# VectorE's program in the first part of a one-core decoder trunk: an order from a play-through of all recorded operations in place of the scheduler's own

## The chip, the cores and the metric

The kernel runs on one core of one Trainium2 chip. A core has five engines that each work through a program of their own: TensorE (PE) for matmuls and its weight loads (PEld), VectorE (DVE), ScalarE (ACT), GpSimd (POOL) and SyncE (SP), which here mostly starts DMA transfers. They wait for one another through semaphores. The metric is the device time of one execution in microseconds (us), the median of several runs.

## The reference

One inference step of a decoder layer for two groups of requests that share the weights: one prompt of 1024 tokens, and 8 samples of 8 tokens each. Cut to what matters:

```python
h = rms_norm(x) * (1 + sc) + sh                       # adaLN of the condition c
P = h @ w_in                                          # 1024 -> 1792 rwkv + 512 pool + 2048 gate columns
r, k, v, xw, xa, xg = split(pr + (pr_prev - pr) * mu) # token shift
decay = exp(-exp(-softplus(-(w0 + tanh(xw) @ w2)) - 0.5))
# per head (8 heads of 64), per token:
S = S * decay + (S @ -kk) (kk * a)^T + v k^T          # 64 x 64 state
y = S @ r                                             # then group norm, bonus, gate g
o_p = grouped causal means over windows 2, 4, 8, 16, minus the token, @ pool_w
merged = sigmoid(g_r) * (y @ w_br_rwkv) + sigmoid(g_p) * (o_p @ w_br_pool)
x = x + gate * (merged @ w_out)
x = x + gate2 * (square(relu(adaLN(x) @ w_ff1)) @ w_ff2)
y = rms_norm(x)
```

All is float32. The new states (shift, pool and rwkv) are outputs too.

## The kernel before, in words

Features lie on the 128 partitions and tokens on the free axis: 1024 prompt tokens and 64 sample tokens make 1088 columns, cut in three chunks of 364, 362 and 362 for the matmuls. Large products are made of three matmuls in the type fp32r: an operand is split in a rounded part and a rest (`whi`/`wlo` for weights, pairs of `hx` rows for activations), and `mm3` adds hi·hi, hi·lo and lo·hi in PSUM. A weight block `wraw` (128x512) is loaded by SP, ACT makes `whi` of it, DVE makes `wlo = wraw - whi`; the first product with a `wlo` so waits for DVE.

The span has three stages. Up to about 95 us the condition's modulation, the norm and the first rows are made. From about 95 to 750 us runs `phase1`, the first part. Then `phase2` does the merge, `w_out`, and the MLP.

In `phase1` two kinds of work share PE. The **background** is a stream of projections (`stream`, `products`): for each block of columns of `w_in` it issues 8 x 3 x 3 matmuls into PSUM tiles of the tag `mm`; ACT and DVE evacuate them to rows `px`, then `d` (token shift) and to scratch in DRAM (`d_x`, `d_th`). The **foreground** are chains of small steps for four pairs of heads, f = 0 to 3:

- `front` and `ra`: k, kk, a, the decays by a scan along 64-token pieces (`wt`, `e`, `bk`, `ra`);
- `scores` (`unit`): the 64x64 products inside each piece (`ab`, `at`, `ak`), transposes of v (`uv`, loaded from `d_x` with 32x32 blocks exchanged);
- `inverse` and `level`: the inverse of a triangular 64x64 matrix for each piece, by a serial chain of fifteen pairs of DVE operations (`hv`, `tt`), then transposes (`iv`, `hv`) and small matmuls `w<-iv,hv`;
- `affine`, then `chain`: the state `S` goes through 16 pieces; at each, PE does `wc<-S,ra`, DVE does one small update `S<-S,end,wc`, and PE needs that `S` for the next;
- `sample` (the 8 x 8 sample tokens) and `post` (group norm by `w<-wt,bones`, reciprocals, bonus, gate).

The order of PE is written out when the program is built: `Pace.run` draws from the background and lets in a step of the foreground when a model of the engines (`Clocks`) says that its operands are there. Inside `manual_schedule(engines={PE})` PE keeps that order. DVE, ACT, POOL and SP are ordered by the tile scheduler, which takes instructions in its own view of readiness.  All DVE, ACT, POOL and SP operations go through the wrapper `Engine.__getattr__`, so in the profile before they all show the wrapper's line L187; PE's matmuls show L359.

Buffers come in rings of few places (`hv`, `iv`, `wt`, `ra`, `S` with 3, PSUM tag `mm` with 4, `w` and `wc` with 2): an operation that writes a new tile also waits until the old tile at that place has been read.

Of the kernel before, what the change touches and what calls it, by code (L numbers as in the profile page):

```python
# [10 lines left out]
F32R = mybir.dt.float32r  # L11
# [67 lines left out]
class Clocks:  # L79
# [5 lines left out]
    def __init__(self, pace):  # L85
        self.pace, self.on = pace, False
        self.busy = {"vector": [], "scalar": [], "gpsimd": [], "sync": []}
        self.seen, self.slots, self.table = {}, {}, 0

    def region(self, ap):  # L90
# [82 lines left out]


class Engine:

# [4 lines left out]
    def __getattr__(self, op):  # L181
        f = getattr(self.real, op)

        def g(*a, **kw):
            if self.c.on:
                self.c.op(self.name, op, a, kw)
            return f(*a, **kw)  # L187

        return g
# [11 lines left out]
class Pool:  # L201
# [5 lines left out]
    def tile(self, *a, **kw):  # L207
        t = self.pool.tile(*a, **kw)
        if self.c.on and kw.get("tag") and kw["tag"] not in self.free:
            self.c.new(kw["tag"], kw["bufs"], t)  # L210
        return t
# [110 lines left out]
class K:  # L322
# [27 lines left out]
    def mm(self, out, lhsT, rhs, **kw):  # L350
        n, mode = math.prod(rhs.shape[1:]), tuple(32 if v <= 32 else 64 if v <= 64 else 128 for v in (lhsT.shape[0], math.prod(lhsT.shape[1:])))
        if mode != self.mode:
            self.pace.t += 150 if self.clocks.on else 200
# [4 lines left out]
        self.product(out, lhsT, rhs)  # L358
        return self.nc.tensor.matmul(out, lhsT, rhs, **kw)  # L359

# [21 lines left out]
    def tr(self, out, in_, ident):  # L382
        if self.mode != (P, P):
            self.pace.t += 150 if self.clocks.on else 200
        self.mode = (P, P)
        if self.clocks.on:
            self.pace.t = max(self.pace.t, self.clocks.ready(in_), self.clocks.touch(out, False))
        self.pace.t += 2 * math.prod(ident.shape[1:]) / 2.4 + 3
        self.product(out, in_)
        self.nc.tensor.transpose(out, in_, ident)  # L390

# [1063 lines left out]
    def phase1(self, ctx):  # L1455
# [41 lines left out]
        self.orr = [[None] * 4 for _ in range(2)]  # L1497
        self.clocks.on = True
        self.pace.split = lambda: self.mode != (P, P)
        self.pace.run(back, [self.chains(), self.heads(), self.pools(), self.or_rows()])  # L1500
        self.clocks.on = False
        self.pace.split = lambda: True
        nc.scalar.dma_start(io["o_ns"], self.ns)
# [705 lines left out]
```

## Time and profile before

| | us |
|---|---|
| median of 3 runs (lowest, highest) | 1596.3 (1594.35, 1600.01) |
| profiled execution, its own time | 1603.45 |
| its span | 1601.7 |
| PE busy | 1536.2 (96%) |
| DVE busy | 1109.6 (69%) |
| ACT busy | 664.1 (41%) |
| POOL busy | 151.4 (9%) |

The rows of a profile name an instruction by line, engine, operation and tiles (`out<-in`, buffer numbers left out). "Idle before" is the time for which the engine had nothing to run ahead of that instruction, and the arrow names what ended it. In a table of windows the columns are the window, its length, the busy time of PE, PEld, DVE, ACT and POOL with the number of instructions, then the mean granted clock of PE (1.00 is full speed), the share of the DMA engines and GB/s. A list of a stretch in order of time gives start, duration, engine, and at the end in brackets the idle time before. The profiled execution took 7 us longer than the median of the runs.

### The profile page before, as it was taken

The page shows a single profiled execution, that of the slowest core. Times are in us where ns is not written, and L with a number is a line of the kernel's source. Part 1 is how long each engine was busy: PE and PEld are TensorE (multiplying, and loading weights), DVE is VectorE, ACT ScalarE, POOL GpSimd, SP SyncE. Part 2 cuts the span into 40 slices and gives each one's busy share as a digit, 9 for nine tenths or more (in the row PEclk, how much of TensorE's full clock was granted, in tenths as well). Part 3 has the DMA queues.
Part 4 walks back from the last instruction along what each step waited for, and adds up shares of the span by engine and source line. Part 5 has one row for each costly group of instructions (what it writes and reads, how often), then busy time and mean ns, then how long its engine had stood idle before and what let it go on. Part 6 is the DMA issues. An engine that isn't in the chain of part 4 may idle for free.

```text
span 1601.7 us, 34054 instructions
## 1 busy us (share of the span) xinstructions
PE 1536.2 (96%) x13777; PEld 1445.8 (90%) x13777; DVE 1109.6 (69%) x1944; ACT 664.1 (41%) x1287; POOL 151.4 (9%) x234
## 2 busy tenths in 40 slices
PE   4999999999998999999999999999999999999997
PEld 2998888988898879989899999999999999999997
DVE  5575658775877487536543797998767796666776
ACT  5454364455334543523222573222334344334652
POOL 3100000000000000012510120000000050000000
PEclk9999999999999999999999999999999999999998
DMA  9142523233333343855875555666445996664654
GB/s 363 62 135 76 181 84 112 80 131 128 95 127 119 99 125 119 304 198 179 305 270 188 194 170 198 226 212 206 144 151 202 400 350 197 210 195 160 227 175 144
DMA packets 136399, 290.05 MB, mean 181 GB/s; under 512 B 36881, under 2 KB 40977, under 8 KB 136241
## 3 DMA queue, kind: packets, MB, share of 16 engines
q1 hardware_dynamic: 129856, 266.75, 48.4%
q10 hardware_dynamic: 4320, 14.00, 2.7%
q0 software_dynamic: 2064, 7.13, 1.3%
q8 instruction: 108, 1.77, 0.4%
q14 instruction: 51, 0.41, 0.1%
HBM read 210.54 MB, written 77.28 MB: 180 GB/s over the span
## 4 chain that ended last, share of the span: by engine, by line
PE 79%; DVE 9%; DMA 6%; issue 2%; ACT 2%; SPq 1%; POOL 0%; DVEq 0%; ACTq 0%; POOLq 0%
PE mm L359 52%; PE w L359 13%; PE wc L359 13%; DVE wt L187 2%; DVE hx L187 2%; DMA hid<-in_w_ff 1%; DVE wlo L187 1%; SPq L187 1%; DMA mg<-in_w_ff 1%; DMA wt<-d_x 1%; DMA hid<-in_w_ada_mlp 1%; DVE hv L187 1%; DMA uv<-d_x 1%; DMA t<-d_th 1%; PE w L390 1%
## 5 line engine op out<-in xcount | busy, mean ns | idle before, releaser
L359 PE MATMUL mm<-hx,whi 128*128 128x362 f32 (+2 forms) x2944 | 690.3, 322 | 9.6 <-ACT px L187 3.6
L359 PEld LDWEIGHTS mm<-hx,whi 128*128 128x128 f32 x2944 | 497.9, 190 | 34.6 <-issue 12.8
L359 PE MATMUL mm<-hx,wlo 128*128 128x362 f32 (+2 forms) x1472 | 464.2, 315 | 4.5 <-DVE wlo L187 3.7
L359 PEld LDWEIGHTS mm<-hx,wlo 128*128 128x128 f32 x1472 | 279.6, 190 | 4.7 <-DVE wlo L187 4.7
L359 PE MATMUL mm<-mg,whi 128*128 128x272 f32 (+2 forms) x1312 | 248.8, 289 | 1.2 <-ACT whi L187 0.7
L359 PEld LDWEIGHTS mm<-mg,whi 128*128 128x128 f32 x1312 | 205.4, 188 | 6.1 <-issue 3.4
L359 PE MATMUL mm<-mg,wlo 128*128 128x272 f32 (+2 forms) x656 | 188.5, 287 | 0.0
L359 PE MATMUL wc<-hx,whi 128*128 128x272 f32 x896 | 170.4, 288 | 0.0
L187 ACT ACTIVATE whi<-hid 128x512 fp32r<-128x512 f32 x128 | 80.5, 630 | 148.5 <-PE mm L359 56.1
L359 PEld LDWEIGHTS wc<-hx,whi 128*128 128x128 f32 x896 | 140.3, 188 | 0.0
L359 PE MATMUL wc<-hx,wlo 128*128 128x272 f32 x448 | 128.9, 288 | 2.3 <-DVE wlo L187 2.3
L359 PEld LDWEIGHTS mm<-mg,wlo 128*128 128x128 f32 x656 | 123.6, 188 | 0.0
L187 DVE TENSOR_TENSOR wlo<-hid,whi 128x512 fp32r<-128x512 f32 x128 | 87.5, 686 | 41.0 <-ACT whi L187 40.3
L187 DVE TENSOR_TENSOR wlo<-wraw,whi 128x512 fp32r<-128x512 f32 x82 | 58.3, 711 | 66.7 <-ACT whi L187 60.6
L187 ACT ACTIVATE whi<-wraw 128x512 fp32r<-128x512 f32 x100 | 62.6, 627 | 90.6 <-PE mm L359 48.6
L359 PE MATMUL w<-hx,whi 128*128 128x272 f32 (+1 forms) x480 | 97.2, 297 | 0.0
L187 POOL TENSOR_TENSOR hx<-hx,rs 128x64 f32<-128x64 f32 x24 | 36.8, 1534 | 568.6 <-DMA mg<-in_w_ff 374.2
L359 PEld LDWEIGHTS wc<-hx,wlo 128*128 128x128 f32 x448 | 84.2, 188 | 2.8 <-DVE wlo L187 2.8
L359 PEld LDWEIGHTS w<-hx,whi 128*128 128x128 f32 x480 | 77.3, 189 | 1.0 <-issue 1.0
L359 PEld LDWEIGHTS mm<-mg,hx 128*128 128x128 f32 x576 | 72.8, 188 | 5.0 <-issue 5.0
L359 PE MATMUL mm<-mg,hx 128*128 128x272 f32 (+2 forms) x576 | 74.7, 289 | 0.0
L187 ACT ACTIVATE px<-mm 128x362 f32<-128x362 f32 (+3 forms) x113 | 46.3, 434 | 63.0 <-PE mm L359 56.4
(289 smaller groups left out, 2323.3 us busy)
## 6 DMA issues: line engine op xcount, KB each, us to landing
t<-d_t SPq DMA_DIRECT2D x56, 544.0 KB, 5.0
hid<-in_w_ff SPq DMA_DIRECT2D x110, 256.0 KB, 4.1
d_t<-hx SPq DMA_DIRECT2D x102, 272.0 KB, 2.5
hid<-in_w_ff SPq DMA_DIRECT2D x42, 512.0 KB, 3.8
wraw<-in_w_in SPq DMA_DIRECT2D x68, 256.0 KB, 2.8
mg<-in_w_ff SPq DMA_DIRECT2D x58, 256.0 KB, 5.4
hid<-in_w_ada_mlp SPq DMA_DIRECT2D x24, 512.0 KB, 5.7
d_th<-px SPq DMA_DIRECT2D x22, 544.0 KB, 3.0
```

The costliest lines, as they stand in the source:

```text
L187: return f(*a, **kw)
L359: return self.nc.tensor.matmul(out, lhsT, rhs, **kw)
L390: self.nc.tensor.transpose(out, in_, ident)
```

## The change

While the first part is being built, a new object `Ledger` records every operation of all five engines: the engine, the instruction, a duration, the earlier operations on which it depends (by overlapping regions of the same tile), and the ring buffers that it uses. After the last operation of the first part, `schedule` plays them all through in time. PE takes its operations in the order given. Each other engine takes, of the operations whose operands and buffers are there when it becomes free, the one recorded first. DMA transfers, table loads of ACT and the rings have times and limits of their own in it. Durations are short formulas in the size of an operation. Of the orders that come out, only DVE's is used: `fix` puts a dependency without a semaphore between each two neighbours, so that the tile scheduler must keep DVE in that order. PE's order is as before. ACT, POOL and SP are still ordered by the tile scheduler, which now works around the pinned DVE.

```diff
+import heapq
...
+        self.ledger = Ledger()
...
+class Ledger:
...
+    WAIT = {"tensor": 55, "gpsimd": 60}
+    OVER = {"vector": 80, "scalar": 95, "gpsimd": 60}
+
+    def __init__(self):
+        self.ops, self.seen, self.home, self.ring, self.uses, self.first = [], {}, {}, {}, {}, {}
+        self.base = {}
...
+    def begin(self):
+        self.base = {k: len(names) for k, (_, names) in self.ring.items()}
+
+    def tile(self, name, key, bufs):
+        self.home[name] = key
+        self.ring.setdefault(key, (bufs, []))[1].append(name)
...
+    def cost(self, eng, op, out, ins, a):
+
+        n = math.prod(out.shape[1:])
+        m = max([n] + [math.prod(x.shape[1:]) for x in ins])
+        full = [x for x in ins if math.prod(x.shape[1:]) > 1]
+        cols = len(ins) - len(full)
+        if "dma" in op:
+            return 380
...
+        if op == "reciprocal":
+            return 100 + 6.3 * n
+        if op == "transpose":
+            return 711 * n / 512 if out.shape[0] == 64 or "PSUM" in str(ins[0].space) else 1080
...
+        return 150 + 1.05 * n + 60 * (cols > 0)
...
+    def add(self, eng, ins, ns, out, reads, extra=0):
+
+        i, before = len(self.ops), set()
+        for x, writes in [(x, False) for x in reads] + [(out, True)]:
+            w, a, b, c, d = r = self.region(x)
+            seen = self.seen.setdefault(x.tensor.name, [])
+            for j, (v, p, q, m, n), wrote in seen:
+                if (writes or wrote) and (v != w or p < b and a < q and m < d and c < n):
+                    before.add(j)
+            seen.append((i, r, writes))
+        before.discard(i)
+        names = list(dict.fromkeys(x.tensor.name for x in [out] + reads))
+        for x in names:
+            if x in self.home:
+                self.uses.setdefault(x, []).append(i)
+                self.first.setdefault(x, i)
+        self.ops.append((eng, ins, ns, before, [x for x in names if x in self.home], extra))
...
+    def schedule(self):
+
+        ops = self.ops
+        n = len(ops)
+        engines = ("tensor", "vector", "scalar", "gpsimd", "sync")
+        left, after, follow = [0] * n, [[] for _ in range(n)], [[] for _ in range(n)]
+        for i, (eng, _, _, before, _, _) in enumerate(ops):
+            for j in before:
+                if not eng == ops[j][0] == "tensor":
+                    left[i] += 1
+                    after[j].append(i)
...
+        def enter(i):
+            if ops[i][0] == "tensor":
+                left[i] = -1
+                return
+            t, key = clear(i)
+            if t is None:
+                parked[key].append(i)
+                return
+            ready[i] = max(ready[i], t)
+            heapq.heappush(queue[ops[i][0]], (ready[i], i))
...
+        for _ in range(n):
+            while True:
+                best = None
+                if stands and left[stands[-1]] == -1:
+                    i = stands[-1]
+                    t, _ = clear(i)
+                    if t is not None:
+                        best = max(free["tensor"] + ops[i][5], max(t, ready[i]) + 55), "tensor", i
+                for e in engines[1:]:
+                    w = self.WAIT.get(e, 35)
+                    while queue[e] and queue[e][0][0] + w <= free[e]:
+                        heapq.heappush(pool[e], heapq.heappop(queue[e])[1])
+                    t = free[e] if pool[e] else queue[e][0][0] + w if queue[e] else math.inf
+                    if best is None and t < math.inf or best is not None and t < best[0]:
+                        best = t, e, pool[e][0] if pool[e] else None
+                t, e, i = best
+                if i is not None:
+                    break
+                free[e] = t
+            _, _, ns, _, names, extra = ops[i]
+            if e == "tensor":
+                stands.pop()
+                end, free[e] = t + ns + 180, t + ns
+            elif e == "sync" or extra > 99:
+                heapq.heappop(pool[e])
+                if len(landed) > 7:
+                    t = max(t, landed[-8])
+                free[e] = t + 380
+                served = end = max(t + 1680, served) + extra / 400
+                landed.append(end)
+            else:
+                heapq.heappop(pool[e])
+                if e == "scalar" and extra not in (0, table):
+                    t, table = t + 1283, extra
+                end = t + ns
+                free[e] = end - self.OVER[e]
+            order[e].append(i)
...
+        return order
+
+    def fix(self, tc, eng):
+
+        line = [self.ops[i][1] for i in self.schedule()[eng]]
+        for a, b in zip(line, line[1:]):
+            tc.add_manual_dep(b, a.name, mybir.DependencyInfo(mybir.DependencyClass.NoSync, mybir.DependencyReason.DATA), reason="order")
...
-            return f(*a, **kw)
+            r = f(*a, **kw)
+            if self.c.on:
+                out, *ins = [x for x in list(a) + list(kw.values()) if hasattr(x, "tensor")]
+                ledger = self.c.ledger
+                ledger.add(self.name, r.ins, ledger.cost(self.name, op, out, ins, a), out, ins, math.prod(out.shape) * 4 if "dma" in op else Clocks.TABLE.get(a[2], 0) if op == "activation" else 0)
...
+        if kw.get("tag"):
+            self.c.ledger.tile(t.tensor.name, (id(self), kw["tag"]), kw["bufs"])
...
-        return self.nc.tensor.matmul(out, lhsT, rhs, **kw)
+        r = self.nc.tensor.matmul(out, lhsT, rhs, **kw)
+        if self.clocks.on:
+            ledger = self.clocks.ledger
+            ledger.add("tensor", r.ins, ledger.product(mode, n, rhs.dtype), out, [lhsT, rhs], 92 if mode != was else 0)
...
         self.clocks.on = True
+        self.clocks.ledger.begin()
         self.pace.split = lambda: self.mode != (P, P)
         self.pace.run(back, [self.chains(), self.heads(), self.pools(), self.or_rows()])
         self.clocks.on = False
+        self.clocks.ledger.fix(tc, "vector")
         self.pace.split = lambda: True
```

DVE has the same 1944 instructions as before. Pinned are 813 of them, from about 99 to 740 us; 417 of these change place, most by one to three places, some by twenty or thirty. The wrapper's line becomes L391.

The first place is on DVE near 121 us, in the front and the scores of the first pair of heads. `wlo_1130` is the rest of a weight block of the background; `uv` are the transposed v; `wt`, `ra`, `bk` and `d` are rows of the front and of the token shift. Before, the last rows up to `wlo_1130`:

```order
L187 SCALAR_TENSOR_TENSOR d_1071<-px_935,part,d_1071 128x1024
L187 SCALAR_TENSOR_TENSOR ds_1072<-px_935,part,d_1071 128x64
L187 STREAM_TRANSPOSE uv_1482<-uv_1482 64x8x64
L187 SCALAR_TENSOR_TENSOR ra_1478<-wt_707,e_1021 128x8x64
L187 TENSOR_TENSOR ra_1478<-wt_1019,e_1021 128x8x64
L187 SCALAR_TENSOR_TENSOR ra_1392<-wt_707,e_1021 128x64
L187 TENSOR_TENSOR ra_1392<-wt_1019,e_1021 128x64
L187 STREAM_TRANSPOSE uv_1482<-uv_1482 64x8x64
L187 TENSOR_TENSOR bk_1025<-wt_706,wt_911 64x9x64 x2
L187 SCALAR_TENSOR_TENSOR bk_1025<-wt_912,wt_911 64x9x64 x2
L187 TENSOR_TENSOR wlo_1130<-wraw_1127,whi_1129 128x512
```

And with the change, from the rest of the weight block before it, `wlo_1062`:

```order
L391 TENSOR_TENSOR wlo_1062<-wraw_1059,whi_1061 128x512
L391 SCALAR_TENSOR_TENSOR wt_911<-kscan,wt_911 128x576
L391 SCALAR_TENSOR_TENSOR d_1071<-px_935,part,d_1071 128x1024
L391 SCALAR_TENSOR_TENSOR ds_1072<-px_935,part,d_1071 128x64
L391 SCALAR_TENSOR_TENSOR wt_707<-wt_706,part,wt_707 128x576
L391 TENSOR_SCALAR bk_1025<-wt_912,hp 128x9x64
L391 STREAM_TRANSPOSE uv_1188<-uv_1188 64x8x64
L391 TENSOR_TENSOR wlo_1130<-wraw_1127,whi_1129 128x512
```

The transposes `uv_1482`, the four products `ra` and the four `bk` stood ahead of `wlo_1130` and stand behind it now; a scan, a product and a small `bk` come between the two `wlo`.

The second place is on DVE near 575 us, in the front of the last pair of heads, while the state chain of the third pair runs. `S_6326` and `S_6401` are two neighbouring updates of the state; `ra_6411<-wt_6352,...` needs the row `wt_6352`, which SP loads. Before:

```order
L187 SCALAR_TENSOR_TENSOR S_6326<-S_6257,end_4470,wc_6018 128x64
L187 SCALAR_TENSOR_TENSOR ra_6411<-wt_6135,e_6354 128x8x64
L187 TENSOR_TENSOR bk_6358<-wt_6134,wt_6250 64x8x64
L187 SCALAR_TENSOR_TENSOR bk_6358<-wt_6251,wt_6250 64x8x64
L187 TENSOR_TENSOR bk_6358<-wt_6134,wt_6250 64x8x64
L187 SCALAR_TENSOR_TENSOR bk_6358<-wt_6251,wt_6250 64x8x64
L187 TENSOR_SCALAR wt_6250<-wt_6250 128x576
L187 TENSOR_SCALAR bk_6358<-wt_6251,hp 128x9x64
L187 TENSOR_TENSOR ra_6411<-wt_6352,e_6354 128x8x64
L187 SCALAR_TENSOR_TENSOR S_6401<-S_6326,end_4470,wc_6367 128x64
```

With the change:

```order
L391 SCALAR_TENSOR_TENSOR S_6326<-S_6257,end_4470,wc_6018 128x64
L391 TENSOR_TENSOR wt_6134<-wt_6134,bk_6358 128x512
L391 SCALAR_TENSOR_TENSOR wt_6251<-wt_6251,wt_6135 128x512
L391 SCALAR_TENSOR_TENSOR ra_6411<-wt_6135,e_6354 128x8x64
L391 TENSOR_TENSOR bk_6358<-wt_6134,wt_6250 64x8x64 x2
L391 SCALAR_TENSOR_TENSOR bk_6358<-wt_6251,wt_6250 64x8x64 x2
L391 TENSOR_TENSOR hv_6436<-uv_4930,kct 128x512
L391 SCALAR_TENSOR_TENSOR S_6401<-S_6326,end_4470,wc_6367 128x64
```

The second `ra_6411`, with the two `TENSOR_SCALAR` before it, now comes after `S_6401`; two `wt` rows that stood before `S_6326` now stand behind it, and `hv_6436` comes between.

The third place is on ACT near 494 to 510 us, in the inverse of the third pair: `iv_5612` is a spread copy of the inverse's result `tt`, `wt_5289<-w,eps` evacuate the variance in the group norm of the second pair, `wt_5289<-wt_5289` is its square root, `px_5597<-mm` evacuates the background, and ACT_TABLE_LOAD is ACT's change to another function table. ACT isn't pinned; the tile scheduler ordered it around DVE. Before:

```order
L187 ACTIVATE iv_5612<-tt,kct 128x32x16
L187 ACTIVATE wt_5289<-w_5494,eps 128x364
L187 ACTIVATE wt_5289<-w_5500,eps 128x362
L187 ACTIVATE wt_5289<-w_5509,eps 128x362
L187 ACTIVATE px_5103<-w_5522,part 128x364
L187 ACTIVATE px_5103<-w_5529,part 128x362
L187 ACTIVATE whi_5544<-wraw_5542 128x512
L187 ACT_TABLE_LOAD
L187 ACTIVATE wt_5289<-wt_5289 128x1088
L187 ACT_TABLE_LOAD
L187 ACTIVATE px_5597<-mm_5462 128x364
```

With the change:

```order
L391 ACTIVATE wt_5289<-w_5494,eps 128x364
L391 ACTIVATE wt_5289<-w_5500,eps 128x362
L391 ACTIVATE wt_5289<-w_5509,eps 128x362
L391 ACTIVATE iv_5612<-tt,kct 128x32x16
L391 ACTIVATE px_5103<-w_5522,part 128x364
L391 ACTIVATE px_5103<-w_5529,part 128x362
L391 ACTIVATE whi_5544<-wraw_5542 128x512
L391 ACTIVATE px_5597<-mm_5462 128x364
L391 ACTIVATE px_5597<-mm_5463 128x362
L391 ACTIVATE whi_5586<-wraw_5584 128x512
L391 ACTIVATE px_5597<-mm_5464 128x362
L391 ACT_TABLE_LOAD
```

`iv_5612` stands behind the three `wt_5289<-w,eps` now, and the table load and `wt_5289<-wt_5289` behind the three `px_5597`.

More of the change, by code (lines that the diff above doesn't have):

```diff
@@ L186, in g @@
                 self.c.op(self.name, op, a, kw)
-            return f(*a, **kw)
+            r = f(*a, **kw)
[3 more added lines that the diff above has]
+                ledger.add(self.name, r.ins, ledger.cost(self.name, op, out, ins, a), out, ins, math.prod(out.shape) * 4 if "dma" in op else Clocks.TABLE.get(a[2], 0) if op == "activation" else 0)
+            return r
         return g
@@ L351, in mm @@
         n, mode = math.prod(rhs.shape[1:]), tuple(32 if v <= 32 else 64 if v <= 64 else 128 for v in (lhsT.shape[0], math.prod(lhsT.shape[1:])))
-        if mode != self.mode:
+        was = self.mode
+        if mode != was:
             self.pace.t += 150 if self.clocks.on else 200
@@ L358, in mm @@
         self.product(out, lhsT, rhs)
-        return self.nc.tensor.matmul(out, lhsT, rhs, **kw)
+        r = self.nc.tensor.matmul(out, lhsT, rhs, **kw)
+        if self.clocks.on:
+            ledger = self.clocks.ledger
+            ledger.add("tensor", r.ins, ledger.product(mode, n, rhs.dtype), out, [lhsT, rhs], 92 if mode != was else 0)
+        return r
     def took(self, n, mode):
@@ L387, in tr @@
             self.pace.t = max(self.pace.t, self.clocks.ready(in_), self.clocks.touch(out, False))
-        self.pace.t += 2 * math.prod(ident.shape[1:]) / 2.4 + 3
+        ns = 2 * math.prod(ident.shape[1:]) / 2.4 + 3
+        self.pace.t += ns
         self.product(out, in_)
-        self.nc.tensor.transpose(out, in_, ident)
+        r = self.nc.tensor.transpose(out, in_, ident)
+        if self.clocks.on:
+            self.clocks.ledger.add("tensor", r.ins, 267, out, [in_, ident])
     def weights(self, src):
```

80 lines of the change are left out of this document (added).

## The prediction

> **What bounds the kernel now.** I read the page first, for the busy engine; then the windows, for the part that the change touches; then the waits of TensorE (PE), for what a better order of VectorE (DVE) can give back at all.
>
> ```profile
> span 1601.7 us, 34054 instructions
> PE 1536.2 (96%) x13777; PEld 1445.8 (90%) x13777; DVE 1109.6 (69%) x1944; ACT 664.1 (41%) x1287; POOL 151.4 (9%) x234
> 95.00:760.00 665.00, 639.46 (x6887) 576.11 (x6886) 453.00 (x837) 289.60 (x607) 50.85 (x117) 0.99 0.40 134
> 760.00:1601.00 841.00, 825.72 (x6486) 809.93 (x6484) 606.79 (x1043) 325.19 (x606) 80.29 (x66) 0.99 0.62 216
> ```
>
> PE is the bound. In the first part (95 to 760 us; columns: length, then busy time of PE, weight load, DVE, ACT, POOL) it is busy 639.46 of 665.00 us. So 25.5 us of idle PE is the most that any order of the other engines can win there, apart from the clock, below. The second part keeps its program: a gain or loss of the first should pass through it as it is, since PE is busy 825.72 of 841.00 us there.
>
> ```profile
> PE wc L359 <- DVE S L187: 8.3, 6, 2.6
> PE mm L359 <- DVE wlo L187: 3.7, 2, 3.3
> PE mm L359 <- ACT px L187: 3.6, 3, 3.1
> PE mm L359 <- DVE px L187: 1.4, 1, 1.4
> ```
>
> These are total, number and longest of PE's waits by releaser. The six on `S` (the recurrent state's update), the long ones on `wlo` and on the two `px` make most of the 25.5. The rest is short, or follows a chain whose next link needs PE itself; no reordering of DVE removes that.
>
> **The change, part by part.** It adds no instruction and takes none away; 813 DVE instructions of the first part are pinned, and about half change place. So every term is a wait of PE, and the question is always the same: by how much does the DVE operation at its end come earlier?
>
> *The gap before `wlo`.*
>
> ```profile
> 117.77 0.69 DVE L187 STREAM_TRANSPOSE uv<-uv 64x512 f32<-64x512 f32 x1
> 122.23 1.52 DVE L187 SCALAR_TENSOR_TENSOR bk<-wt,wt 64x576 f32<-64x576 f32 x2
> 123.79 0.69 DVE L187 TENSOR_TENSOR wlo<-wraw,whi 128x512 fp32r<-128x512 f32 x1
> 124.53 0.43 PE L359 MATMUL mm<-hx,wlo 128*128 128x364 f32 x1 [3.30 <-DVE wlo L187]
> ```
>
> From 117.77 to 123.79 DVE runs ten operations (two `uv` transposes, four `ra`, four `bk`), and every one of them falls behind `wlo_1130` in the new order. Of those before them three come new between it and the `wlo` ahead and two leave, about 1 us more, so `wlo` comes some 5 to 6 us earlier. The gap is 3.30. It closes: **-3.3**.
>
> *The state updates.*
>
> ```profile
> 406.23 0.33 PE L359 MATMUL wc<-S,ra 64*64 64x64 f32 x4 [1.15 <-DVE S L187]
> 406.40 0.28 PE L359 MATMUL wc<-ra,S 64*64 64x64 f32 x4
> 411.39 0.28 DVE L187 SCALAR_TENSOR_TENSOR S<-S,end,wc 128x64 f32<-128x64 f32 x1
> 411.73 0.69 PE L359 MATMUL wc<-ab,uv 128*64 128x64 f32 x16 [1.42 <-DVE S L187]
> 576.93 0.69 DVE L187 TENSOR_TENSOR ra<-wt,e 128x512 f32<-128x512 f32 x1 [0.64 <-DMA wt<-d_x]
> 577.54 0.27 DVE L187 SCALAR_TENSOR_TENSOR S<-S,end,wc 128x64 f32<-128x64 f32 x1
> 577.87 0.33 PE L359 MATMUL wc<-S,ra 64*64 64x64 f32 x4 [2.61 <-DVE S L187]
> 227.51 0.71 DVE L187 STREAM_TRANSPOSE uv<-uv 64x512 f32<-64x512 f32 x1 [1.39 <-DMA uv<-d_x]
> 229.18 0.33 PE L359 MATMUL wc<-S,ra 64*64 64x64 f32 x4 [1.70 <-DVE S L187]
> ```
>
> At 406.68 PE has what the next `S` (0.28 us) needs; DVE reaches it at 411.39, since seven operations of `bk`, `wt` and `hv` stand between two updates. In the new order three do: some 3 us earlier, and the gaps of 1.15 and 1.42 close. At 577 the update stands behind a product (`ra`) that waits 0.64 us for its load; the new order puts the product and the two operations before it behind `S`. By the timeline these end 2.5 us after the point where `S` could have run, so of 2.61 about 2.5 goes. At 227 nothing moves: `S` still stands behind transposes whose load lands at 227.5, so its 1.70 stays. The other two gaps of the six hold 8.3 - 1.15 - 1.42 - 2.61 - 1.70 = 1.4; their `S` moves by about as much, of which I take 1.1. Sum: 1.15 + 1.42 + 2.5 + 1.1 = **-6.2**.
>
> *The gap before `px`.*
>
> ```profile
> 491.38 1.24 DVE L187 SCALAR_TENSOR_TENSOR px<-px,px 128x1024 f32<-128x1024 f32 x1
> 492.65 1.20 ACT L187 ACTIVATE px<-mm 128x364 f32<-128x364 f32 x3 [1.61 <-DVE px L187]
> 493.18 0.60 PE L359 MATMUL mm<-hx,whi 128*128 128x362 f32 x2 [3.12 <-ACT px L187]
> 493.73 0.74 ACT L187 ACTIVATE iv<-tt,kct 128x512 f32<-128x512 f32 x1
> 499.61 0.56 ACT L187 ACTIVATE wt<-w,eps 128x362 f32<-128x362 f32 x1 [0.24 <-PE w L359]
> 498.95 7.01 DVE L187 RECIPROCAL wt<-wt 128x182 f32<-128x182 f32 x6 [1.50 <-ACT wt L187]
> 515.64 0.97 PE L359 MATMUL w<-iv,hv 32*32 32x32 f32 x90 [0.19 <-DVE hv L187]
> ```
>
> ACT empties PSUM only once DVE's `px` is done at 492.62. Nine operations go from ahead of that `px` to behind it, over 4 us of work, so the 3.12 closes. But it is lent, not given. At 515.64 PE waits again, for `hv`, and already has no slack there (0.19). In the new ACT order `iv` (493.73 now) stands behind the third `wt<-w,eps`, which ends at 500.17 now, or about 497.0 when PE is 3.1 us ahead. Then `iv` 0.74, one transpose of about 1.1, and the six reciprocals of 7.0 us end at 497.0 + 0.7 + 1.1 + 7.0 = 505.8, where they end at 505.96 today. What is behind them gains only because ACT does three `px` evacuations ahead of a table load rather than behind it, and that is half eaten by an `iv` transpose (1.0) put later. From both sides: -0.9 (all returned, and some wait beside) to +3.1 (nothing returned); I take 0.9 gained, **-0.9**.
>
> *The gap at 724, and one new one at 638.*
>
> ```profile
> 725.19 0.60 PE L359 MATMUL mm<-hx,whi 128*128 128x362 f32 x2 [1.43 <-DVE px L187]
> 637.77 0.60 PE L359 MATMUL w<-wt,bones 128*128 128x362 f32 x2
> ```
>
> The `px` at 724 passes reciprocals, 2.4 us by their durations, and closes its 1.43: **-1.4**. At 637.77 PE has no gap now. Its operand is the product `wt<-w,wt` of the norm, and the new order puts steps of the inverse (`hv`, `tt`) before that product; laid out with the durations of the trace it ends 1.3 us later, and PE has no slack for it: **+1.3**.
>
> *The clock.*
>
> ```profile
> 353.48 1.64 PE L359 MATMUL w<-z,hv 32*32 32x32 f32 x64 [1.14 <-ACT hv L187]
> 353.92:357.33 3.41, 3.41 (x54) 2.81 (x49) 3.22 (x8) 1.65 (x4) 0.00 (x0) 0.50 0.43 98
> 125.22:128.64 3.42, 3.42 (x22) 2.80 (x21) 3.42 (x5) 1.11 (x1) 0.76 (x2) 0.50 0.63 173
> 493.86:497.28 3.42, 3.42 (x13) 3.42 (x12) 2.99 (x4) 0.60 (x1) 0.00 (x0) 0.50 0.39 163
> 579.20:582.61 3.41, 3.41 (x16) 1.30 (x16) 3.41 (x9) 2.56 (x6) 1.20 (x2) 0.50 0.02 3
> 408.30 1.08 PE L359 MATMUL w<-hv,ab 128*64 128x512 f32 x4
> 579.60 1.98 PE L359 MATMUL w<-hv,ab 128*64 128x512 f32 x4
> ```
>
> The granted clock (third number from the right) is 0.50 for 3.41 us soon after each of these gaps. The same four matmuls take 1.98 us there and 1.08 at full clock. One stretch so costs between 0.9 (these four alone) and 1.98 to 1.08 carried over its 3.41 us, 1.55. I take 1.2. Where the gaps at 121 and 575 close, two stretches go: **-2.4**. The one at 494 counts for nothing, since 515 takes its gain back.
>
> The Trainium skill, "TensorE: Matmul & The Clock Gate", section "HAM oscillation — how this bites in real kernels", says in short that PE idle gaps of more than about 3.4 us throttle the clock. No gap here is that long, and by that rule the clock term would be nil, and the forecast 2.4 us higher. The trace does not agree: a gap of 1.14 us was followed by a stretch at 0.50.
>
> *Sum:* -3.3 - 6.2 - 0.9 - 1.4 + 1.3 - 2.4 = **-12.9 us**. Against the profiled execution's own 1603.45 us that is 1590.6. That execution lies 7 us above the median of the runs shown (1596.3, 1594.35 to 1600.01); since the terms are differences, I carry the sum to the median: 1583.4. The DVE operations that made way come later and some will be late somewhere that I did not find, so I say **1584**. Its own range is 1578 to 1591: below, all of the 490 gap and the longer clock price (-2.2 - 1.1 - 1.4 for 638); above, the low ends of `px`, of the clock, and two more waits like that at 638.
>
> **The rivals.**
>
> *The stalls only move.* DVE does the same 453 us of work in the first part, and PE's own chains end on it. What happened to the 490 gap by my working (lent 3.1, kept 0.9) may happen to the others too: the 121 gap at the inverse behind it, that at 575 at the next updates. If three quarters is returned, about 3 us stays: 1593. That the order makes no difference at all belongs here too: 1596. For it: `hv` at 515.64 with 0.19. Against it: after 121, PE's next wait on DVE of over 1 us is at 227, and that one is a load's.
>
> *Slower: DVE at the head of its line.* The new order was played with fitted landing times of loads; the engine takes it as written. A transpose whose load is late then holds every `S` and `wlo` behind it.
>
> ```profile
> L187 DVE STREAM_TRANSPOSE uv<-uv 64x512 f32<-64x512 f32 x16 | 11.3, 704 | 10.1 <-DMA uv<-d_x 9.9
>   DMA uv<-d_x: 9.9, 6
> ```
>
> Of the 16 `uv` transposes in the first part six wait for their load today (the second row is from the trace's answer on that tile), 9.9 us in all, 1.65 each; the one at 227 passed 1.70 of it to PE. The price is thus 1.7 a time. It cancels the gain from eight more such waits (12.9 / 1.65 = 7.8), and is slower by more than 0.3% from eleven. There are only ten others; all ten would give 1596.3 - 12.9 + 16.5 = 1600, and with the gain of the S gaps lost with them, 1606. So 1602 as this case's time. For it: the new order does put operations ahead of others by modelled times, as at 638. Against it: at 577 it did the contrary, moving `S` ahead of an operation that waits for a load.
>
> The Trainium skill, "TensorE: Matmul & The Clock Gate", section "Architectural detail: the array is 16× 32×32, not 1× 128×128", says that DVE and ACT run strictly first in, first out and only PE reorders. The row at 227.51 agrees: `S` waited behind it. The rule is what makes this rival possible; it gives no size.
>
> *More than I add up.* Gaps that I call fixed shorten too, because PE's lead reaches ACT and the loads: 20 us of the 25.5 and three clock stretches, 1596.3 - 20 - 3.6 = 1573.
>
> **How the numbers follow.** The forecast 0.60, stalls that move 0.18, slower 0.13, more 0.09. What a measurement of this kernel can tell from no change is about 0.3%, 4.8 us: faster is below 1591.5, slower above 1601.1. The forecast's range lies within faster; with the larger gain and a little of the first rival that gives 0.71. Same is the rest of that rival and the mild end of the slower one, 0.18; slower 0.11. The range reaches from 1576, which leaves out most of the larger gain, to 1598, which takes in the first rival and leaves out the slower one: 1576 to 1598.
>
> **What would show it.** In the changed kernel's profile: PE's waits on `S` from 8.3 to about 2 us, with the one near 227 left; no wait on `wlo` of 3 us near 121; idle of PE in the first part from 25.5 to about 15; no stretch at 0.50 near 125 and 579; the wait on ACT's `px` near 490 gone, but a longer one for `w<-iv,hv` near 512; a new one of about 1.3 on `wt` near 630. The prediction is wrong if PE's idle time in the first part stays above 22 us, or falls and the second part grows by as much, or if new waits of PE on `wlo`, `hv` or `wt` in the inverse sum to more than 6 us.

## The result, and the profile after

| | before | with the change |
|---|---|---|
| median, us (lowest to highest, 11 runs each) | 1600.01 (1594.35 to 1604.17) | 1588.57 (1584.52 to 1593.74) |
| ratio of the medians' runs, 95% interval | | 0.9933 (0.9915 to 0.9951) |
| profiled execution, own time / span | 1603.45 / 1601.7 | 1584.52 / 1582.7 |

The change makes the kernel 11.4 us faster, 0.7%. Forecast were 12.9 us. The absolute forecast, 1584, lies 4.6 us under the median, mostly because the kernel before came out at 1600.0 in eleven runs and not at 1596.3 as in the first three. The profiled pair differs by more, 18.9 us: the profiled execution of the changed kernel is the fastest of its eleven, that of before lies above its median. So the pair's rows show where time went, but not the size of the typical gain.

The page of the changed kernel, its first rows:

```profile
span 1582.7 us, 34027 instructions
PE 1527.7 (97%) x13777; PEld 1438.4 (91%) x13777; DVE 1112.0 (70%) x1944; ACT 663.6 (42%) x1287; POOL 149.1 (9%) x234
```

Its windows, with the columns as before. The first holds the same matmuls as 95.03 to 760.04 us of before; the second follows a gap at 343.9; the third is its only stretch at half clock in the first part.

```profile
94.11:743.06 648.95, 633.15 (x6887) 570.42 (x6886) 455.61 (x837) 289.80 (x607) 46.88 (x117) 1.00 0.42 138
343.80:350.00 6.20, 5.05 (x85) 4.47 (x85) 4.89 (x10) 3.63 (x7) 1.55 (x2) 1.00 0.28 66
395.91:399.32 3.41, 3.41 (x12) 2.38 (x13) 2.25 (x4) 0.28 (x1) 0.00 (x0) 0.50 0.30 96
```

The first part takes 648.95 us where it took 665.0: 16.1 us. PE's idle time in it falls from 665.0 - 639.5 = 25.5 to 648.95 - 633.15 = 15.8, by 9.7. The other 6.4 us are in PE's busy time: the same matmuls in 633.15 us for 639.5, most of it since one stretch at half clock is left of five (four stretches are about 5 us at the price worked out under "The clock"). Of the rest of the pair's 18.9 us, 0.9 come before 95 us and the remaining 1.9 behind 743 us, where all five engines have the same order in both.

PE's waits that answer to those shown of before:

```profile
PE wc L571 <- DVE S L391: 0.7, 1, 0.7
PE mm L571 <- DVE wlo L391: 0.4, 1, 0.4
PE mm L571 <- ACT px L391: 0.8, 2, 0.4
PE w L571 <- DVE hv L391: 2.3, 2, 1.5
PE w L571 <- DVE wt L391: 1.5, 1, 1.5
PE w L571 <- ACT iv L391: 2.1, 3, 0.9
```

The waits on `S` fall from 8.3 to 0.7, on `wlo` from 3.7 to 0.4, on ACT's `px` from 3.6 to 0.8. The last three are new or have grown: in the first part they were 1.0, nothing and 0.3 before. The larger of the waits that are left stand at these places (start, duration, and at the end the idle time before):

```profile
129.06 0.48 PE L571 MATMUL w<-ra,bk 64*128 64x128 f32 x2 [0.86 <-ACT iv L391]
130.45 0.82 PE L571 MATMUL w<-ra,bk 64*128 64x128 f32 x9 [0.90 <-ACT iv L391]
221.62 0.33 PE L571 MATMUL wc<-S,ra 64*64 64x64 f32 x4 [0.74 <-DVE S L391]
345.03 1.16 PE L571 MATMUL w<-z,hv 32*32 32x32 f32 x61 [1.15 <-ACT hv L391]
501.24 0.95 PE L571 MATMUL w<-iv,hv 32*32 32x32 f32 x89 [1.52 <-DVE hv L391]
621.31 0.59 PE L571 MATMUL w<-wt,bones 128*128 128x362 f32 x2 [1.52 <-DVE wt L391]
```

At 501 and 621 the forecast waits are there. Those at 129 and 130 were not forecast.

### The profile page after: what moved, and what is told of

It is laid out like the page before. It is cut to its first block, busy times and chain, and to the rows that moved or that the text cites. A ratio compares the mean times of both kernels' runs of the same rounds, so it can differ in the third digit from the quotient of the medians.

```text
span 1582.7 us, 34027 instructions
## 1 busy us (share of the span) xinstructions
PE 1527.7 (97%) x13777; PEld 1438.4 (91%) x13777; DVE 1112.0 (70%) x1944; ACT 663.6 (42%) x1287; POOL 149.1 (9%) x234
## 4 chain that ended last, share of the span: by engine, by line
PE 79%; DVE 8%; DMA 7%; ACT 3%; issue 2%; SPq 0%; POOL 0%; DVEq 0%; ACTq 0%; POOLq 0%
PE mm L571 53%; PE w L571 13%; PE wc L571 13%; DMA hid<-in_w_ff 2%; DVE hx L391 2%; DVE wt L391 1%; DVE wlo L391 1%; DMA mg<-in_w_ff 1%; DMA hid<-in_w_ada_mlp 1%; DVE mg L391 1%; DMA t<-d_t 1%; DMA t<-d_th 0%; DMA x<-in_xT 0%; DVE hv L391 0%; PE w L607 0%
## 5 line engine op out<-in xcount | busy, mean ns | idle before, releaser
L391 ACT ACTIVATE whi<-hid 128x512 fp32r<-128x512 f32 x128 | 80.3, 630 | 145.9 <-PE mm L571 53.3
L391 DVE TENSOR_TENSOR wlo<-hid,whi 128x512 fp32r<-128x512 f32 x128 | 87.9, 689 | 40.6 <-ACT whi L391 39.5
L391 DVE TENSOR_TENSOR wlo<-wraw,whi 128x512 fp32r<-128x512 f32 x82 | 58.1, 709 | 64.5 <-ACT whi L391 59.0
L391 ACT ACTIVATE whi<-wraw 128x512 fp32r<-128x512 f32 x100 | 62.6, 627 | 84.8 <-PE mm L571 52.6
L391 POOL TENSOR_TENSOR hx<-hx,rs 128x64 f32<-128x64 f32 x24 | 36.8, 1532 | 570.0 <-DMA mg<-in_w_ff 356.8
L571 PE MATMUL w<-hx,wlo 128*128 128x272 f32 (+1 forms) x240 | 70.7, 295 | 0.5 <-DVE wlo L391 0.5
```

The source lines that it names most:

```text
L391: r = f(*a, **kw)
L571: r = self.nc.tensor.matmul(out, lhsT, rhs, **kw)
```

## The experiments

All kernels below but two are built in one way: a list of instruction numbers takes the place of the order that the play-through finds, and VectorE is pinned to it.

```diff
-        line = [self.ops[i][1] for i in self.schedule()[eng]]
+        own = {o[1].name: o[1] for o in self.ops if o[0] == eng}
+        line = [own[f"I-{k}"] for k in LINE if f"I-{k}" in own]
```

PE's order is the same in all runs. ACT, POOL and SP are not pinned, so the moves shift some of their operations as well (ACT's order differs from before's at 8 places in h_s, 42 in h_core and 91 in the change; SP's at 0, 15 and 35): a difference in time comes from the moves together with what the scheduler makes of them. In h_s2, a_rep and a_rep2 it also orders some 40 VectorE operations of the second part anew, near 1290 to 1330 us; PE passes that stretch (1270 to 1345 us of before) in 75.0 us in every profile, so no cost of this shows. Runs whose name begins with h have before's list with some operations moved, those with a the changed kernel's. The ratio is to the kernel before on the same chip. "Moved" counts the operations that are taken out and set in elsewhere. It isn't the 417 of the change, which counts places: operations that are passed change place too. To make the change's order out of before's, at least 181 operations have to be moved; in h_core 130 places differ. "First part" is the time between the two matmuls that stand at 95.03 and 760.04 us before; "gaps" sums PE's gaps of 0.25 us and more there; "half clock" is the time there at a granted clock of 0.50, all three worked out from the one profile that each run has.

| run | moved | ratio (95%) | first part | gaps | half clock |
|---|---|---|---|---|---|
| before | | 1 | 665.0 | 24.7 | 17.1 |
| b_again, the same kernel | | | 663.2 | 22.1 | 20.5 |
| the change | 181 or more | 0.9933 (0.9915 to 0.9951) | 649.0 | 15.2 | 3.4 |
| h_wlo | 1 | 0.9992 (0.9975 to 1.0009) | 656.7 | 20.9 | 6.8 |
| h_s | 4 | 1.0011 (0.9993 to 1.0028) | 669.4 | 24.6 | 27.3 |
| h_px | 6 | 0.9982 (0.9964 to 1.0000) | 662.8 | 20.5 | 27.3 |
| h_all | 11 | 0.9968 (0.9955 to 0.9981) | 656.1 | 20.9 | 6.8 |
| h_s2 | 15 | 1.0039 (1.0022 to 1.0056) | 662.1 | 23.2 | 13.6 |
| h_all2 | 22 | 0.9991 (0.9972 to 1.0010) | 658.6 | 20.0 | 13.6 |
| h_core | 41 | 0.9895 (0.9869 to 0.9920) | 644.7 | 11.7 | 3.4 |
| a_undo | 10 back | 1.0018 (0.9995 to 1.0040) | 663.4 | 24.8 | 17.1 |
| a_rep | 7 more | 0.9936 (0.9918 to 0.9954) | 651.2 | 15.2 | 6.8 |
| a_rep2 | 3 more | 0.9917 (0.9890 to 0.9944) | 647.3 | 13.5 | 3.4 |
| a_flat | all anew | 1.0138 (1.0113 to 1.0163) | 685.1 | 37.2 | 44.4 |

### The named waits, alone and together

h_wlo moves `wlo_1130`, h_s four updates of `S`, h_px the two groups of `px`, and h_all all eleven:

```diff
+wlo_1130<-wraw_1127,whi_1129 128x512                 (h_wlo)
 uv_1482<-uv_1482 64x8x64 ... ten operations
-wlo_1130<-wraw_1127,whi_1129 128x512
...
+S_4504<-S_4472,end_2687,wc_4194 128x64               (h_s, one of four)
 wt_4370<-kscan,wt_4370 128x576 ... six operations
-S_4504<-S_4472,end_2687,wc_4194 128x64
...
+px_5103<-px_5102,px_5103 128x1024                    (h_px, one of two groups)
 wt_5291<-wt_5289,wt_5290 128x364 ... seven operations beside two small zf that move too
-px_5103<-px_5102,px_5103 128x1024
```

> Of the eleven moves only wlo_1130, ten places forward. Theory A: the gap of 3.30 us near 121 goes, in the trace PE is 3 to 4.5 us earlier from there on, to the end; about 3 us in the median. Theory B: the ten operations behind it are 0.6 us later each, the next waits of PE on VectorE (near 130 and 185) take the 3 us back; 0 to 1 us in the median.

> Of the eleven moves only the four updates of S. Theory A: the gaps of 0.97, 1.15, 1.42 and 2.61 us go, 5 to 7 us in the trace and in the median. Theory B: what stands behind them (products of the front) makes PE wait in the scores; 0 to 2 us.

> Of the eleven moves only the two px groups. By the prediction's step on the gap before px: the 3.12 near 490 goes but about 2.2 of it comes back as a wait for w<-iv,hv some 20 us later, and the 1.43 near 724 goes: 2 to 3 us in all. Theory B': nothing comes back, 4.5 us. Theory C: all comes back and the inverse, which the px now delays by 1.2 us, adds to it: 0 to 1 us.

> The kernel before with its own VectorE order written out, and eleven operations moved forward in it: wlo_1130 ahead of the transposes uv_1482 (ten places), the four updates S_2730, S_4472, S_4504 and S_6401 (two to six places), px_5103 with its two small zf products (ten places), the three px_8105 ahead of two reciprocals. All other VectorE operations stay where they were. Theory A (the gain is that of the named waits, one by one): the gaps of 3.30, 0.97, 1.15, 1.42, 2.61, 3.12 and 1.43 us close, with part of the 3.12 returned at w<-iv,hv; 9 to 14 us faster than before, as much as the whole change. Theory B (the gain comes from the order as a whole, and single stalls only move to the next chain): under 5 us.

Measured: the four updates alone bring nothing (ratio 1.0011), `wlo` alone nothing that can be told (0.9992), `px` about 3 us at the edge of what can be told (0.9982), all together 5 us (0.9968; the interval is 3 to 7 us), half of the change. So theory A (9 to 14) is out, and theory B (under 5) is neither shown nor excluded. The rows show why. In h_s, PE's gaps at 405 and 410 are gone, and the updates come at once. VectorE then, in order of time:

```profile
411.37 0.69 DVE L438 SCALAR_TENSOR_TENSOR ra<-wt,e 128x512 f32<-128x512 f32 x1
...
414.79 1.51 DVE L438 TENSOR_TENSOR bk<-wt,wt 64x576 f32<-64x576 f32 x2
416.33 0.28 DVE L438 SCALAR_TENSOR_TENSOR S<-S,end,wc 128x64 f32<-128x64 f32 x1
```

And on PE:

```profile
409.82 0.28 PE L618 MATMUL wc<-ra,S 64*64 64x64 f32 x4
...
416.67 0.33 PE L618 MATMUL wc<-S,ra 64*64 64x64 f32 x4 [2.40 <-DVE S L438]
...
582.56 0.48 PE L618 MATMUL wc<-S,ra 64*64 64x64 f32 x4 [2.63 <-DVE S L438]
```

PE has the next update's operand at 410; VectorE reaches that update at 416.33, behind the same products as before. The 2.57 us that were won at 405 and 410 stand as 2.40 at the next update; the 2.61 at 575 as 2.63 one update on. In h_px the first gap (3.12) is gone, and 20 us later there is a new one:

```profile
512.52 0.91 PE L618 MATMUL w<-iv,hv 32*32 32x32 f32 x56 [2.18 <-DVE hv L438]
```

That is the return of 2.2 us that the prediction worked out for this place. In h_wlo, 3.30 went and 0.46 and 0.90 came 8 us later, at the two `w<-ra,bk` that wait in the changed kernel too.

### Following the wait

h_s2 moves eleven more updates of the same chains, h_all2 adds `wlo` and `px` to that.

```diff
+S_4571<-S_4504,end_2687,wc_4537 128x64
 ra_4579<-wt_4465,e_4467 128x8x64 ... six operations
-S_4571<-S_4504,end_2687,wc_4537 128x64
...
+S_6445<-S_6401,end_4470,wc_6367 128x64
 wt_6250<-kscan,wt_6250 128x576 ... four operations
-S_6445<-S_6401,end_4470,wc_6367 128x64
```

> The kernel before with fifteen updates of S moved forward: the four of the run that moved S alone, and eleven of their neighbours in the same three chains (S_2503 to S_2800, S_4571, S_4619, S_6326, S_6445, S_6467; one to eight places). Theory A' (a stall of the chain that is closed alone reappears at the next update, since the same products of the front still stand ahead of that one; only when each update in the row passes them is the time won): the waits of 2.40 us near 414 and 2.63 near 580 of that run are gone, PE's waits on S sum to under 3 us, 4 to 6 us faster than before. Theory B (the front's products, pushed back by the updates, become the wait): PE waits for the scores of the next head pair instead, 0 to 2 us.

> The same fifteen updates of S, and wlo_1130 and the two px groups moved forward as well: twenty-two operations in all, everything else of VectorE as before. Theory A': 9 to 12 us faster than before, that is nearly all that the change gained. Theory C (the gain of the change also needs the several hundred other small moves): it stays at 5 to 7 us, as with the eleven moves.

Measured: h_s2 is slower than before (1.0039), h_all2 the same (0.9991); theory A' is wrong, and B right in kind. PE's waits on `S` do fall, to 3.0 us in h_s2. But PE then waits for the scores, whose results VectorE has to evacuate. VectorE in h_s2, in order of time:

```profile
419.06 0.28 DVE L438 SCALAR_TENSOR_TENSOR S<-S,end,wc 128x64 f32<-128x64 f32 x1
419.52 1.29 DVE L438 TENSOR_TENSOR wt<-wt,wt 128x1088 fp32r<-128x1088 f32 x1 [0.18 <-ACT wt L438]
420.73 0.68 DVE L438 TENSOR_TENSOR wlo<-wraw,whi 128x512 fp32r<-128x512 f32 x1
421.33 1.23 DVE L438 TENSOR_TENSOR d<-px 128x1038 f32<-128x1038 f32 x1
...
422.74 0.42 DVE L438 TENSOR_TENSOR ab<-w,kct 128x256 f32<-128x256 f32 x1
```

ACT, which copies parts of the scores behind VectorE's `at`, and PE:

```profile
423.57 0.27 ACT L438 ACTIVATE iv<-w 32x128 f32<-32x128 f32 x1 [4.09 <-DVE at L438]
424.34 0.49 PE L618 MATMUL w<-ra,bk 64*128 64x128 f32 x2 [2.56 <-ACT iv L438]
```

The evacuations `ab` and `at` stand behind a long `wt` product, a `wlo` and a long `d` product; ACT's copies come after them, the PSUM tiles of the scores are not free until then, and PE waits 2.56 us. In h_s2 the same is worth 1.54 at 588. (Why h_s2 is not the same as before but 4 to 6 us slower is not settled: its profiled execution, 1597.14 us, is the fastest of its twelve, and shows no further wait. The mean granted clock of its twelve, 0.988 against 0.989 for before on that chip, makes about 1 us of it.)

h_core takes that step as well: the twenty-two moves of h_all2 (with `S_2730` one place further), and nineteen more.

```diff
+ab_4673 at_4675 ab_4673 at_4675 (four evacuations; the same at 128 and 586 us)
 wt_4665<-wt_4262,wt_4664 128x1088 ... wlo_4707, d_4718, psm_4719
-ab_4673 at_4675 ab_4673 at_4675
...
-uv_5031<-uv_5031 64x8x64 (two; with two ra the same at 586 us)
 wlo_4604, wt_4262, S_4657, ab_4673, at_4675 ...
+uv_5031<-uv_5031 64x8x64
...
+hv_5689<-w_5624,kct 128x512
 wt_5287<-wt_5287,wt_5694 128x1088
-hv_5689<-w_5624,kct 128x512
```

> The kernel before with forty-one VectorE operations moved: the twenty-two of the run before (wlo_1130, fifteen S, the px groups), and nineteen more where that run showed the wait again: three groups of score evacuations (ab, at; four each) ahead of long row products, four transposes uv and two small ra behind them, hv<-w ahead of a long wt product. Theory D (the gain comes from a few dozen operations: those that PE waits for pass the long rows that nobody waits for, in the whole chain of front, scores and state at once): PE's gaps in the first part fall from 24.7 to 14 to 16 us, 8 to 12 us faster than before. Theory C (the gain needs the many small moves too): gaps stay at 18 to 20 us and the time at 3 to 6 us faster.

Measured 0.9895: 1583.1 against 1602.0 us, that is 17 us by the ratio (13 to 21) and 19 by the medians. So it is theory D in kind, with more gained than its 8 to 12 us. Forty-one moved operations do at least as much as the change's order. That they do more is not shown: the two were not timed side by side, and a_rep2, the changed kernel with three repairs, reached 0.9917 (0.9890 to 0.9944) on the chip of h_core. Which of the nineteen further moves carry the gain was not tested one by one; twelve of them are the evacuations of the scores. The place at 412 us in h_core, on VectorE:

```profile
411.05 1.35 DVE L438 SCALAR_TENSOR_TENSOR wt<-wt,part,wt 128x1088 f32<-128x1088 f32 x1
412.31 0.28 DVE L438 SCALAR_TENSOR_TENSOR S<-S,end,wc 128x64 f32<-128x64 f32 x1
412.50 0.42 DVE L438 TENSOR_TENSOR ab<-w,kct 128x256 f32<-128x256 f32 x1
...
414.05 1.45 DVE L438 STREAM_TRANSPOSE uv<-uv 64x512 f32<-64x512 f32 x2
```

And the window that holds h_core's first part:

```profile
94.40:739.10 644.70, 632.40 (x6887) 571.19 (x6886) 451.33 (x836) 290.37 (x607) 50.77 (x117) 1.00 0.42 138
```

`ab` runs right behind `S`, the transposes and the long product that nobody waits for come later, and PE has no gap from 365 to 503 us of half a microsecond or more. Over the first part (the window) its idle time is 644.7 - 632.4 = 12.3 us.

### Taking the same operations out of the change

a_undo moves ten operations of the changed kernel back:

```diff
-wlo_1130, S_2730, S_4472, S_4504, S_6401, px_5103 (with its copy), px_8105 (three)
 ... the operations that stood ahead of each before
+wlo_1130, S_2730, S_4472, S_4504, S_6401, px_5103 (with its copy), px_8105 (three)
```

> The changed kernel, with wlo_1130, S_2730, S_4472, S_4504, S_6401, px_5103 (with the small copy behind it) and the px_8105 moved back behind the operations that stood ahead of each before; the other updates of S and all else in the new order. If the named waits carry the gain, the waits near 121, 405, 490, 575 and 724 come back and 6 to 9 us of the change's 11 are lost. If the rest of the order carries it, under 3 us are lost.

Measured: 1.0018. The whole 11 us are lost, more than either theory said. The waits come back, that on `wlo` with 1.7 of its 3.3 us, and one is longer than it was:

```profile
PE wc L618 <- DVE S L438: 7.2, 5, 2.3
PE mm L618 <- ACT px L438: 6.1, 3, 5.6
PE mm L618 <- DVE wlo L438: 3.3, 3, 1.7
```

The wait for `px` is 5.6 and not 3.1: ahead of the place to which `px_5103` went back VectorE now waits twice for ACT's `wt` (0.90 and 0.96 us), and one more product of 0.54 stands there. So this run overstates what the ten are worth by some 2.5 us. Still: without them the other moves of the change gain about 3 us at most.

### Repairs of the new order

a_rep moves the score evacuations near 127, two `wt<-w,wt` near 621 and `hv<-w` near 500 forward in the changed kernel; a_rep2 only the last three.

```diff
+wt_7051<-w_7125,wt_7051 128x364
+wt_7051<-w_7132,wt_7051 128x362
 tt<-hv_6995 128x2x14
 hv_6995<-hv_6994,tt 128x450
-wt_7051<-w_7125,wt_7051 128x364
-wt_7051<-w_7132,wt_7051 128x362
```

> The changed kernel with seven VectorE operations moved forward, one group at each wait that the new order made: the four evacuations of the scores (ab, at) near 127 us ahead of three long row operations; two wt<-w,wt near 621 ahead of a reduction and a product of the inverse; hv<-w near 500 ahead of a long wt product. If these waits are local and not given back later: 0.9 + 0.9 + 1.1 + 1.2 = about 4 us faster than the changed kernel, 15 faster than before. If each only moves to the next step of the inverse or the scores: 0 to 1 us.

> The changed kernel with three VectorE operations moved forward: the two wt<-w,wt near 621 and hv<-w near 500; the score evacuations, whose move made a wait of 2.15 us elsewhere, stay. Local waits of 1.1 and 1.2 us go: 2 us faster than the changed kernel in the trace's gaps; the median may not tell it (its interval is about 3 us).

Measured: a_rep 0.9936, the same as the change, so the 4 us did not come; a_rep2 0.9917. The gap at 621 is gone in both, and 0.3 us is left of the one at 501. In a_rep PE waits at the next group of scores instead, whose evacuations VectorE reaches only at 133.41, behind long rows, `ra` products and transposes:

```profile
135.01 1.15 PE L618 MATMUL w<-kct,ra 64*64 64x64 f32 x32 [2.15 <-ACT iv L438]
```

That is 2.15 us for the 0.86 and 0.90 that were removed: once more a wait that only moved. a_rep2 has the smaller sum of gaps, 13.5 against 15.2. Its median lies 2.6 us under the changed kernel's, but the intervals overlap, so that is not shown.

### The durations in the play-through

```diff
+        if eng == "vector":
+            return 557
         if op == "reciprocal":
             return 100 + 6.3 * n
```

> The changed kernel's play-through with one duration, 557 ns (the mean of all VectorE operations of the first part), for every VectorE operation in place of the fitted ones. If the rule (oldest recorded of the ready ones first) does the work: within 4 us of the changed kernel. If the fitted durations do it: more than half of the 11 us lost, since long rows (1.1 to 1.3 us) are then taken as cheap as a state update (0.28).

Measured: 1.0138, 21 us slower than before and 32 slower than the change. With one duration for all, the rule makes the kernel slower; its gain hangs on durations that tell long rows from short ones. PE's waits in a_flat:

```profile
PE wc L573 <- DVE S L393: 12.2, 8, 3.9
PE w L573 <- DVE hv L393: 11.4, 5, 3.9
PE mm L573 <- DVE wlo L393: 6.6, 3, 5.1
```

The longest wait for `wlo` stands at the very place that the change cleared. VectorE there, and then PE:

```profile
113.78 0.71 DVE L393 STREAM_TRANSPOSE uv<-uv 64x512 f32<-64x512 f32 x1 [2.94 <-DMA uv<-d_x]
```

```profile
120.81 0.67 PE L573 MATMUL mm<-hx,wlo 128*128 128x364 f32 x1 [5.11 <-DVE wlo L393]
```

VectorE waits 2.94 us for a load at the head of its line, with a backlog behind it. That is the prediction's slower rival, with its mechanism, in an order whose model of time is off. How much of the 21 us comes from such loads was not followed further.

### The clock

b_again is the kernel before, unchanged, profiled a second time, on another chip.

> The kernel before itself once more, for its profile. If the half-clock stretches follow from the length of the gaps, they stand at the same five gaps of the first part as in the first profile. If they hang on where a gap falls in a window that runs by itself, the gaps are the same to 0.3 us and the stretches stand elsewhere, or are more or fewer; the first part is then longer or shorter by about 1.5 us for each stretch of 3.4 us.

PE near 354 us, and two windows with the granted clock third from the right:

```profile
354.42 1.20 PE L359 MATMUL w<-z,hv 32*32 32x32 f32 x64 [1.14 <-ACT hv L187]
```

```profile
353.92:357.33 3.41, 2.91 (x73) 2.64 (x74) 3.32 (x8) 2.55 (x5) 0.82 (x1) 1.00 0.31 102
123.80:130.63 6.83, 5.60 (x27) 4.98 (x28) 6.68 (x10) 1.35 (x3) 1.11 (x2) 0.50 0.50 147
```

The gap of 1.14 us before `w<-z,hv` is there again, but the clock stays at 1.00 behind it, and the 64 matmuls take 1.20 us for 1.64. The gap near 121 (3.51 this time) is followed by 6.83 us at half clock and not by 3.41. In the changed kernel the gap of 1.15 at 345 has no stretch behind it either (window 343.80:350.00 above). The gaps themselves were not all the same to 0.3 us: that near 575 is 1.88 this time and not 2.61. So a gap makes a stretch likely, and its place in time decides. Every stretch of the first part in the fourteen profiles of the table is 3.41 or 6.83 us long.

The traces show how the place decides. In each profile all stretches start a whole number of steps of 3.413 us apart (in that of before, 67 steps lie between 125.22 and 353.92). Cut into such steps, the fourteen first parts hold 23 steps at full clock with more than 1.84 us of idle PE, and each was followed by a stretch; of the 167 with 0.58 to 1.84 us 25 were, and of those with less, none. So a gap that is split between two steps can go free: of a wait of 2.40 us in h_s 2.13 fell in one step, and a stretch followed at 417.95; in h_all a wait of 2.40 us was split in 1.40 and 1.00, and none followed.

The price: over the fourteen profiles, the first part less its gaps is 633.1 us and 0.36 us more for each microsecond at half clock (a straight line through them; the furthest profile is 1.8 us off). That is 1.24 us for 3.41.

The Trainium skill, "TensorE: Matmul & The Clock Gate", section "What's actually happening", says that the hardware watches a window of activity that runs by itself. The lengths of the stretches, the steps of 3.413 us and b_again agree with that. The same section gives the half rate after at least one idle window, about 3.4 us. Here gaps of 1.14 us were followed by it, so the measurement decides.

## Why the prediction was right, and where not

**The bound and the size.** PE's idle time in the first part was what there was to win. 12.9 us were forecast, 11.4 measured, and the second part kept the lead. Not every term came out, as the next paragraphs show; that the sum did is partly luck. In the profiled pair the waits gave 9.7 for the 10.5 forecast, and the four stretches about 5 for 2.4. In the medians the clock is an estimated 5 of the 11.4 (last section), which leaves 6 to 7 for the waits; b_again's gaps (22.1 against 15.2) say the same.

**`wlo`, -3.3.** The gap went, but 1.76 us of it came back within 10 us (0.86 and 0.90 at `w<-ra,bk`): `ab` and `at` stand behind what made way. Net -1.5. The first rival's mechanism, at a place where the prediction said that the next wait of over 1 us was at 227.

**The state, -6.2.** In the changed kernel's trace the waits on `S` fall by 7.6. But the step's reasoning failed: it priced each update by the wait at its own place. h_s shows that these four moves win nothing; h_s2, that all updates together win nothing either. What wins is that the evacuations of the scores, and a few transposes and products with them, change places with the long rows as well (h_core). The change does all of these (in its order the fifteen updates stand two to ten places earlier, the evacuations near 412 us eight), so the sum came out right for a reason that the prediction did not have. And the 1.70 at 227, which was to stay, fell to 0.74 though its row kept its place: the load landed earlier against PE there.

**The gap at 490, -0.9.** Right in size: 3.12 went, and 1.52 came at 501 and 0.68 at 493 (`w<-px,plw`, waiting for `d`), together the 2.2 that were expected; h_px shows 2.18 in one wait. But the chain of `iv`, transposes and reciprocals, from which the return was worked out, does not fix it: in a_rep2 `hv<-w` passes one product of 1.27 us, and of the 1.52 only 0.32 is left. That three `px` evacuations come ahead of a table load was given as the reason for the part that is kept; no run tested that.

**724 and 638, -1.4 and +1.3.** The first closed; a gap of 0.71 came there in its place. The second came as forecast, 1.52.

**The clock, -2.4.** The price of a stretch was right (1.2; 1.24 measured). The number of stretches was not: four fewer in the profiled pair where two were forecast, and it hangs on the execution, too. (In the lower end of the range 1.1 stands for the longer price; two stretches at 1.55 in place of 1.2 give 0.7.) Three kernels with nearly the same gaps (h_wlo 20.9, h_px 20.5, h_all 20.9) show 6.8, 27.3 and 6.8 us of them in one execution each. What can be said is that the kernels with few gaps over 1 us (the change 4, a_rep2 1, h_core 4, before 10) show few stretches.

**The rivals.** "The stalls only move" is what single moves do (h_s, a_rep, half of h_px), and not what the whole order does. "VectorE at the head of its line" is seen with poor durations (a_flat). "More than I add up", 23 us, was not reached, by h_core's 17 to 19 neither.

## What to carry to other kernels

A wait of the bounding engine is not worth its length when the operation at its end is moved alone: the backlog that stood ahead of it stands ahead of the next wait. Follow the wait through the chain, one run for each step, until the operations that make way are ones that nobody waits for; forty-one moves found so did at least as much here as the order of a play-through, which takes 181 moves or more. And an order from a play-through is as good as its durations: with one mean duration the same rule cost 21 us.

## What was not expected of the hardware

The same program with nearly the same gaps had its half-clock stretches at other places in a second execution, and a gap of 1.14 us was followed by one in one execution and not in the other. Over kernels with like gaps the stretches differ by 20.5 us (h_px against h_wlo), which at 0.36 is 7 us, two thirds of what the change gains. The executions of the kernel before spread from 1594 to 1607. The mean granted clock of 78 of them is on record: the 29 at 0.990 and more have a median of 1598.3 us, the 20 at 0.987 and less one of 1603.3, so the clock is a part of the spread, and not all of it. It is also a part of the gain: the mean over these 78 is 0.9886, over the eleven of the change 0.9931, about 14 us less at half clock, which by the price of 0.36 is an estimated 5 of the 11.4 us. So one profiled pair doesn't size a change like this; the medians do.
